# Raw weights in whole rows, and loads on other queues, in a hybrid attention and retention layer

## The chip, the core and the metric

The kernel runs on one core of a Trainium2 chip. The core has TensorE (PE, matrix products into PSUM), VectorE (DVE), ScalarE (ACT), GpSimd (POOL) and SyncE (SP), which run side by side and each in its own order, and 16 DMA engines that all queues share. SP, ACT and GpSimd can issue DMAs; an issue is an instruction in the stream of its engine. The metric is the device time of one execution in microseconds, lower is better.

## The reference

One decoder layer over 4096 tokens of width 1024, in float32:

```python
h = rms_norm(x, norm_gain)
proj = h @ w_in                       # 1024 x 3584
qa, ka, va, ga, qr, kr, vr, gr = split(proj, IN_SPLITS)
attn = dilated_attention(qa, ka, va)  # 8 heads x 64, rotary, three branches (128,1) (512,4) (2048,16)
ret = retention(qr, kr, vr)           # 4 heads, chunks of 128, decay, group norm
mixed = concat([silu(ga) * attn, silu(gr) * ret * ret_gn_gain])
out = rms_norm(x + mixed @ w_out, final_gain)
```

## The kernel before, in words

Products keep float32 accuracy by a split: each operand is a high part and a low part (operand minus high part), and three matmuls stand for one. ACT makes the high part, VectorE mostly the low one.

**Stage one** (`phase1`) makes q, k, the attention's v, and the retention's q and k. The columns of `w1` are taken in two passes, each over 8 blocks of 512 tokens: pass 0 (`ps` 0, blocks `q` 0 to 7) gives k and v, pass 1 (blocks 8 to 15) gives q and the retention's part. A block is not one product but seven smaller ones (P1, P5, P6, P3, P7, P2, P4, a scheme of Strassen's kind) from sums of the quarters of weights and of x. The quarters of the weights are A and B (alternate 128 columns), each with an upper half of rows (`Aa`, `Ba`) and a lower one (`Ab`, `Bb`). A product has two banks, thus a block 14 steps (`STEPS`) of 24 matmuls. What is done at which step is a list written by hand: `at(step, fn, ...)` appends a call, `front=True` puts it ahead of the step's others, and the loop at line 758 emits each step's product and then its calls. The order on each engine and queue is the order of these calls.

Before a pass the raw quarters lie in tiles that are free at that time (`ROOM`, line 191); from them `scale_b`, `minus` (GpSimd), `plus_times` (VectorE) and `split_w` make the operands of the seven products, and `HOMES` (line 206) says in which rooms the high and the low part of each are kept. At the start `load_w` (line 228) brings the quarters one by one, in pieces of 128 columns (512 bytes) and some of 256. For pass 1 `load_raw` (line 606) brings all four rows of a quarter with four or eight DMAs of 512-byte pieces, at steps s-13 and s-11 before the pass; the switch is at s = 112.

**The way into stage two** (s = 224): `first_k` loads the first head's K (4096 columns) on GpSimd's queue, `w2_some` the eight tiles of w2 on ACT's queue at s-10 and s-8, `w2_split` splits them, `first_chunk` and `first_chunk_split` bring and split the first two chunks of x, `first_q` loads q. **Stage two** (`phase2`) loads its constants on GpSimd's queue and then runs attention on TensorE, with the values and the retention as a `filler` between its steps; the filler runs alone first (`LEAD`, line 18). **Stage three** gates, projects and normalizes.

Of the kernel before, what the change touches and what calls it, by code (L numbers as in the profile page):

```python
# [24 lines left out]
S = 4096  # L25
# [113 lines left out]
def phase1(tc, io, dr, right, ahead):  # L139
# [5 lines left out]
    with ExitStack() as ctx:  # L145
# [41 lines left out]
        def whole(p, tag):  # L187
# [37 lines left out]
        def pairs_of(rows, c0, part):  # L225
            return rows[:, c0 : c0 + 512].rearrange("k (u t c) -> k t u c", t=2, c=128)[:, part]

        def load_w(ps, dst, part, k):

            rows = io["w1"][k * 128 : (k + 1) * 128, :]  # L230
            halves = [h.rearrange("k (u c) -> k u c", c=128) for h in (dst[:, 0:256], dst[:, 256:512])]
            nc.sync.dma_start(halves[0], pairs_of(rows, 0 if ps else 512, part))
            if ps:
                nc.sync.dma_start(halves[1], pairs_of(rows, 1024, part))
            else:
                nc.sync.dma_start(dst[:, 256:512], rows[:, 1536 + 256 * part : 1792 + 256 * part])
# [14 lines left out]
        def split_w(ps, prod, src, part=None, engine=None, ks=range(4)):  # L251
# [3 lines left out]
            for k in ks:  # L255
                hi, lo = W[ps].hi[prod][k], W[ps].lo[prod][k]
# [162 lines left out]
        def values(q, half):  # L419
# [3 lines left out]
            for i, p in enumerate(parts):  # L423
                for u in range(2):
                    n = 4 * q + 2 * half + u
                    nc.scalar.activation(
                        vf[:, u, 256 * i : 256 * i + 256], p[:, 256 * u : 256 * u + 256], AF.Copy, scale=rs[:, n : n + 1]
                    )
# [177 lines left out]
        def load_raw(name, room, part, k0):  # L606

            raw[name] = ROOM[room](F32)
            for i, t in enumerate(raw[name].tiles):
                n = raw[name].n  # L610
                r0 = (k0 + i * n) * 128
                for u in range(4):
                    c0 = (0, 1024)[u // 2] + 256 * (u % 2) + 128 * part
                    src = io["w1"][r0 : r0 + n * 128, c0 : c0 + 128]
                    nc.sync.dma_start(t[:, :, u * 128 : (u + 1) * 128], src.rearrange("(k p) c -> p k c", p=128))
# [98 lines left out]
        for k in range(4):  # L714
            load_w(0, Ab[k], 0, 4 + k)
# [1112 lines left out]
```

## Time and profile before

| | us |
|---|---|
| median of 3 runs | 2394.1 (2393.79 to 2399.23) |
| the profiled execution | 2397.46 |
| its span, first to last instruction | 2395.7 |
| TensorE busy in the span | 2287.0 (95%) |
| VectorE busy | 1734.7 (72%) |
| ACT busy | 1140.1 (48%) |
| GpSimd busy | 784.7 (33%) |
| mean granted TensorE clock | 0.980 |

Times in rows are us from the first instruction. Stage one lasts until about 739, stage two follows. A releaser (`<-`) is what ended a wait. q1 is SP's DMA queue, q10 ACT's, q0 GpSimd's. `ACTq` or `SPq` is an engine's DMA issue, with the time that it held the stream.

### The profile page before, as it was taken

What the parts mean: (1) busy time and instruction counts of PE and PEld (TensorE: products, weight loads), DVE (VectorE), ACT (ScalarE), POOL (GpSimd) and SP (SyncE); (2) the same over time, 40 slices, a digit from 0 to 9 for tenths busy, and PEclk for the clock granted to TensorE, in tenths of its full rate; (3) what the DMA queues carried; (4) which work ended last, traced back from release to release, by engine and by line L of the source; (5) the groups of instructions that cost most, each with busy time, mean ns of one, the idle gap of its engine ahead of it and who ended that gap; (6) DMA issues with size and microseconds to landing.
All of it is one profiled execution on the core that took longest, in us unless ns stands there. A gap on an engine that the chain in (4) does not pass through costs nothing.

```text
span 2395.7 us, 47366 instructions
## 1 busy us (share of the span) xinstructions
PE 2287.0 (95%) x16808; PEld 2059.8 (86%) x16808; DVE 1734.7 (72%) x4231; ACT 1140.1 (48%) x3082; POOL 784.7 (33%) x965
## 2 busy tenths in 40 slices
PE   5899997999986999999999999998899999999998
PEld 5899997999986888888888888877789999999997
DVE  6686778998976878787887879786655655555654
ACT  4555555332322666667666666667322322322221
POOL 1344443222122535344443535446121121121110
PEclk8999998999998999999999999999999999999999
DMA  6678777545467675858576675755676666666653
GB/s 185 203 234 260 229 239 211 163 153 178 152 184 205 139 171 138 188 125 192 139 167 153 153 165 127 178 136 184 156 185 152 148 169 147 143 171 152 141 156 93
DMA packets 457581, 405.07 MB, mean 169 GB/s; under 512 B 207896, under 2 KB 411800, under 8 KB 452224
## 3 DMA queue, kind: packets, MB, share of 16 engines
q1 hardware_dynamic: 421328, 324.52, 53.5%
q0 software_dynamic: 29968, 58.38, 8.3%
q10 hardware_dynamic: 6048, 19.14, 2.4%
q8 instruction: 133, 2.18, 0.4%
q14 instruction: 104, 0.85, 0.1%
HBM read 283.12 MB, written 118.64 MB: 168 GB/s over the span
## 4 chain that ended last, share of the span: by engine, by line
PE 59%; DVE 3%; DMA 3%; issue 1%; ACT 1%; SPq 1%; POOL 0%; POOLq 0%; DVEq 0%; ACTq 0%
PE S L1036 9%; PE O L1106 7%; PE T L1073 6%; PE po L48 4%; PE po L50 4%; PE po L49 4%; PE g L50 4%; PE g L49 4%; PE g L48 4%; PE V L48 3%; PE V L50 2%; PE V L49 2%; DMA wb<-dr_w 1%; PE Ro L1327 1%; PE Ro L1330 1%
## 5 line engine op out<-in xcount | busy, mean ns | idle before, releaser
L1057 DVE CUSTOM_DVE_ANT_0 S<-S,mask 128x256 f32<-128x256 f32 (+1 forms) x768 | 308.5, 402 | 158.8 <-PE S L1036 125.3
L1064 ACT ACTIVATE P<-S,nm 128x256 f32<-128x256 f32 (+1 forms) x768 | 338.0, 450 | 45.8 <-DVE nm L1057 42.7
L50 PE MATMUL g<-h,wg 128*128 128x256 f32 x1024 | 289.7, 283 | 0.0
L310 ACT ACTIVATE h<-xt 128x1024 fp32r<-128x1024 f32 (+1 forms) x115 | 119.4, 1038 | 240.7 <-DVE xt L302 107.3
L1073 PE MATMUL T<-ident,P 128*128 128x128 f32 x1368 | 213.2, 273 | 0.0
L49 PE MATMUL po<-wo,m 128*128 128x512 f32 x512 | 200.4, 391 | 0.0
L1617 POOL TENSOR_TENSOR rs<-v,mhalf 128x1 f32<-128x1 f32 x32 | 17.5, 547 | 546.6 <-DVE v L1615 527.6
L1106 PE MATMUL O<-pt,v 128*64 128x128 f32 (+1 forms) x1968 | 196.3, 326 | 0.0
L50 PEld LDWEIGHTS g<-h,wg 128*128 128x128 f32 x1024 | 196.2, 192 | 0.0
L1036 PE MATMUL S<-kk,qc 128*128 128x256 f32 x1024 | 187.6, 307 | 7.0 <-issue 2.8
L48 PE MATMUL po<-wohi,m 128*128 128x512 f32 x448 | 178.7, 399 | 6.4 <-ACT m L40 5.4
L1036 PEld LDWEIGHTS S<-kk,qc 128*128 128x128 f32 x1024 | 150.1, 191 | 35.7 <-issue 18.3
L50 PE MATMUL po<-wohi,m 128*128 128x512 f32 x448 | 176.7, 395 | 0.2 <-DVE m L41 0.2
L314 DVE TENSOR_TENSOR h<-xt,h 128x1024 fp32r<-128x1024 f32 (+1 forms) x115 | 138.8, 1207 | 49.5 <-ACT h L310 49.3
L1106 PEld LDWEIGHTS O<-pt,v 128*64 128x64 f32 x1968 | 121.3, 137 | 60.7 <-issue 31.6
L1556 ACT ACTIVATE e<-g 128x256 f32<-128x256 f32 x128 | 48.3, 379 | 256.1 <-PE g L50 239.7
L804 POOL TENSOR_TENSOR hc<-hr,hc 128x512 fp32r<-128x512 f32 x64 | 85.0, 1329 | 241.6 <-ACT hc L803 175.3
L1073 PEld LDWEIGHTS T<-ident,P 128*128 128x128 f32 x1368 | 163.7, 141 | 0.2 <-ACT wg0hi L87 0.2
L1064 ACT ACTIVATION_READ_ACCUMULATOR P<-S,nm 128x1 f32 x768 | 157.5, 205 | 0.0
L40 ACT ACTIVATE m<-e 128x256 fp32r<-128x256 f32 x128 | 53.1, 416 | 209.7 <-DVE e L1563 123.8
L48 PE MATMUL g<-h,wg1hi 128*128 128x256 f32 x512 | 145.2, 285 | 3.1 <-ACT e L1556 3.1
L49 PE MATMUL g<-h,wg1hi 128*128 128x256 f32 x512 | 146.1, 286 | 1.2 <-DVE h L852 1.0
(268 smaller groups left out, 6512.0 us busy)
## 6 DMA issues: line engine op xcount, KB each, us to landing
hr<-in_xT_dram SPq DMA_DIRECT2D x64, 512.0 KB
q<-dr_q SPq DMA_DIRECT2D x128, 256.0 KB
xt<-in_xT_dram POOLq DMA_DIRECT2D x60, 512.0 KB, 8.7
wb<-dr_w SPq DMA_DIRECT2D x128, 192.0 KB
o<-dr_o SPq DMA_DIRECT2D x192, 128.0 KB
v<-dr_v SPq DMA_DIRECT2D x94, 256.0 KB
xn<-in_x_dram ACTq DMA_DIRECT2D x32, 512.0 KB
dr_v<-vo SPq DMA_DIRECT2D x64, 256.0 KB
```

The lines of the kernel that those rows point to most:

```text
L40: nc.scalar.activation(dst[:, 0], src, AF.Copy)
L48: nc.tensor.matmul(out, wh, xh, start=first and i == 0, stop=False)
L49: nc.tensor.matmul(out, wh, xl, start=False, stop=False)
L50: nc.tensor.matmul(out, wl, xh, start=False, stop=last and i == n - 1)
L310: nc.scalar.activation(xs[q, prod][:, 0, ks, :], xq[(q, *SOURCE[prod])][:, ks, :], AF.Copy)
L314: (engine or nc.vector).tensor_tensor(h[:, 1, ks, :], src[:, ks, :], f32(h[:, 0, ks, :]), ALU.subtract)
L804: nc.gpsimd.tensor_tensor(hc[:, :, 1, :], src, hc[:, :, 0, :].bitcast(F32), ALU.subtract)
L1036: nc.tensor.matmul(s[:, j * 256 : (j + 1) * 256], qq[h, t, half][:, off : off + 128] if br == 0 else it["q"][:, t, i, :], rhs, start=(j == ...
L1057: nc.vector.tensor_tensor_reduce(sv, sv, mask[:, it["br"], c0:256], 1.0, BIG, ALU.add, ALU.min, accum_out=nm[:, col : col + 1])
L1064: nc.scalar.activation(it["P", i // 2][:, i % 2, c0:256], sv, AF.Exp, bias=nm[:, col : col + 1], scale=-1.0, accum_out=den[:, col : col + 1])
L1073: nc.tensor.transpose(t[:, j * 128 : (j + 1) * 128], it["P", bank][:, j // 2, j % 2 * 128 : j % 2 * 128 + 128], ident)
L1106: nc.tensor.matmul(o[64 * bank : 64 * bank + 64, c0 : c0 + 128 * m], vt[h, br, idx // 8][:, idx % 8, :], it["pt"][:, a : a + m, :].rearran ...
```

## The change

At the start and before pass 1 the raw weights come in rows of 512 columns (2 KB), A and B side by side in one tile (`Raw`); A and B are then views of it with 128-column pieces (`groups`). The upper halves come first, then the lower ones: for pass 1 at s-12, s-10 and s-8 rather than s-13 and s-11. The value columns of pass 0 are paired in another way, which `values` undoes. The products of pass 1 get other rooms, D lies in another one, and the sum S4 is written over Aa. The scaling of Bb moves from s-7 to s-6, and P1's split goes ahead of the first sum.

At the way into attention w2's loads go to SP's queue, all at s-10, and their splits to s-4 and s-3; K and q are loaded at first only in part (1024 of 4096 and 512 of 2048 columns), the rest on ACT's queue as the filler's first act; the constants go from GpSimd's queue to SP's, at the same place; the loads of x chunks 1 to 3 go from SP's to GpSimd's; and the first two v loads from GpSimd's queue to SP's, in chunk 1.

```diff
             {
-                "P5": ("wh0", "wl0"),
-                "P6": ("wh1", "wl1"),
-                "P3": ("h0", "h1"),
-                "P7": ("q00", "q10"),
-                "P2": ("q01", "q11"),
-                "P4": ("p40", "p41"),
+                "P5": ("wl0", "wl1"),
+                "P6": ("h1", "q10"),
+                "P3": ("h0", "p41"),
+                "P7": ("wh0", "wh1"),
+                "P2": ("q00", "q11"),
+                "P4": ("p40", "q01"),
             },
...
+        def groups(ap):
+            return ap.rearrange("p (g c) -> p g c", c=128)
+        COLS = ((512, 1536), (0, 1024))
+        class Raw:
+            def __init__(self, ps, rooms, k0):
+                self.ps, self.k0 = ps, k0
+                self.tiles = [t[:, i : i + 2, :] for r in rooms for t in ROOM[r](F32).tiles for i in range(0, t.shape[1], 2)]
+                both = [t.rearrange("p q (u t c) -> p (q u) t c", t=2, c=128) for t in self.tiles]
+                self.A, self.B = ([t[:, :, i, :] for t in both] for i in range(2))
+            def load(self, k):
+                for i, c0 in enumerate(COLS[self.ps]):
+                    nc.sync.dma_start(self.tiles[k][:, i, :], io["w1"][(self.k0 + k) * 128 : (self.k0 + k + 1) * 128, c0 : c0 + 512])
...
         def diff_d():
-            raw["D"] = ROOM["q01"](F32)
+            raw["D"] = [groups(t) for t in ROOM["q00"](F32)]
...
-            raw["S4"] = ROOM["q00"](F32)
-            plus_times(raw["S4"], raw["Ab"], 1, raw["Bb"], ALU.add)
+            plus_times(raw["Aa"], raw["Ab"], 1, raw["Bb"], ALU.add)
...
-        at(s - 13, load_raw, "Ba", "wh1", 1, 0, front=True)
-        at(s - 13, load_raw, "Aa", "wh0", 0, 0, front=True)
-        at(s - 11, load_raw, "Ab", "p40", 0, 4, front=True)
-        at(s - 11, load_raw, "Bb", "h0", 1, 4, front=True)
+        at(s - 12, load_raw, "a", range(4), front=True)
+        at(s - 12, open_raw, "a", ("wh0", "wh1"), 0, front=True)
+        at(s - 10, load_raw, "b", (0, 1), front=True)
+        at(s - 10, open_raw, "b", ("p40", "q01"), 4, front=True)
+        at(s - 8, load_raw, "b", (2, 3), front=True)
         at(s - 8, diff_d)
-        at(s - 7, lambda: scale_b(raw["Bb"]))
+        at(s - 6, lambda: scale_b(raw["Bb"]))
+        at(s - 6, split, 1, "P1", "Aa", 0)
         at(s - 6, sum_s1)
-        at(s - 6, split, 1, "P1", "Aa", 0)
...
-            ahead["w2"].load(raw["w2"], js, nc.scalar.dma_start)
+            ahead["w2"].load(raw["w2"], js)
...
-            ahead["kk"] = load_k(nc, kka, dr, 0, nc.gpsimd.dma_start)
+            ahead["kk"] = load_k(nc, kka, dr, 0, nc.gpsimd.dma_start, slice(0, 1024))
...
-            ahead["hr"] = load_x_chunk(nc, hcp, io, 1)
+            ahead["hr"] = load_x_chunk(nc, hcp, io, 1, nc.gpsimd.dma_start)
...
-        at(s - 10, w2_load)
-        at(s - 10, w2_some, (0, 1, 2))
-        at(s - 8, w2_some, (3, 4, 5, 6, 7))
-        for i in range(4):
-            at(s - 6 + i, w2_split, (2 * i, 2 * i + 1))
+        at(s - 10, w2_some, range(8), front=True)
+        at(s - 10, w2_load, front=True)
+        for i in range(2):
+            at(s - 4 + i, w2_split, range(4 * i, 4 * i + 4), front=True)
         at(s - 6, first_chunk)
-        at(s - 3, first_q)
+        at(s - 2, first_q)
         at(s - 2, first_chunk_split)
...
-        Aa, Ab, Ba, Bb = (ROOM[r](F32) for r in ("q11", "p41", "wl0", "h1"))
+        X, Y = Raw(0, ("h1", "q10"), 0), Raw(0, ("q11", "p41"), 4)
+        Aa, Ba, Ab, Bb = X.A, X.B, Y.A, Y.B
         for k in range(4):
-            load_w(0, Aa[k], 0, k)
+            X.load(k)
             load_x(0, 0, 0, k)
         load_x(0, 0, 1)
         for k in range(4):
-            load_w(0, Bb[k], 1, 4 + k)
-            load_w(0, Ba[k], 1, k)
-        load_x(0, 1, 1)
-        for k in range(4):
-            load_w(0, Ab[k], 0, 4 + k)
-        load_x(0, 1, 0)
+            Y.load(k)
+        for half in (1, 0):
+            load_x(0, 1, half)
...
-        for _ in range(2):
-            load_v(*vqueue[vpos[0]], nc.gpsimd.dma_start)
-            vpos[0] += 1
+        def first_loads():
+            load_constants()
+            for i in range(2):
+                load_q(nc, qp, dr, 0, i, 0, nc.scalar.dma_start, slice(512, S // 2), qq[0, i, 0])
+            load_k(nc, kka, dr, 0, nc.scalar.dma_start, slice(1024, S), kk[0])
...
             res = {0: first_rk}
+            first_loads()
             split_rk(first_rk)
...
-                        hraw[c + 1] = load_x_chunk(nc, hcp, io, c + 1)
+                        hraw[c + 1] = load_x_chunk(nc, hcp, io, c + 1, nc.gpsimd.dma_start if c < 3 else None)
```

## Rows read from the trace of the kernel before

**Rows 1.** Windows: busy us (count) of PE, PEld, DVE, ACT, POOL; clock, DMA share, GB/s

```profile
0.00:120.00 120.00, 89.33 (x591) 83.83 (x592) 76.39 (x97) 60.17 (x94) 31.57 (x46) 0.89 0.65 193
...
120.00:360.00 240.00, 238.22 (x1968) 234.65 (x1967) 179.68 (x215) 133.67 (x203) 103.98 (x155) 1.00 0.78 241
...
360.00:420.00 60.00, 45.63 (x309) 44.75 (x308) 48.22 (x65) 31.84 (x50) 22.20 (x32) 0.80 0.71 211
...
700.00:780.00 80.00, 55.01 (x352) 49.38 (x351) 48.66 (x96) 20.88 (x45) 21.93 (x29) 0.85 0.80 203
...
780.00:1300.00 520.00, 518.51 (x4076) 435.79 (x4075) 414.07 (x1545) 358.14 (x1238) 236.35 (x272) 1.00 0.66 155
```

**Rows 2.** Waits of TensorE from 700 to 780: total us, times, longest

```profile
PE V L50 <- POOL hc L804: 8.5, 2, 5.7
...
PE z L402 <- ACT m L410: 6.5, 1, 6.5
...
PE V L48 <- ACT vch L1405: 5.5, 1, 5.5
```

**Rows 3.** Timeline of ACT and VectorE at the end of stage one: start, us, what

```profile
697.87 11.46 ACTq L74 DMA_DIRECT2D w<-in_w_dram  x3
...
709.37 1.09 ACT L410 ACTIVATE m<-z 128x512 f32<-128x512 f32 x2 [10.46 <-DMA dr_r<-or]
...
715.10 5.70 ACTq L74 DMA_DIRECT2D w<-in_w_dram  x4
...
722.85 0.69 DVE L415 TENSOR_TENSOR m<-z,m 128x512 f32<-128x512 f32 x1 [6.35 <-ACT m L410]
```

**Rows 4.** DMA queues from 694 to 704 us: packets, MB, share of 16 engines

```profile
q0 software_dynamic: 178, 1.92, 90.2%
...
q10 hardware_dynamic: 62, 0.13, 5.7%
```

**Rows 5.** Windows at the end of stage one, columns as in rows 1

```profile
703.50:739.30 35.80, 27.07 (x195) 26.59 (x194) 19.20 (x31) 11.24 (x18) 2.58 (x5) 0.86 0.83 223
...
722.80:756.40 33.60, 23.14 (x146) 20.73 (x146) 31.22 (x51) 11.14 (x19) 7.60 (x11) 0.88 0.70 183
```

**Rows 6.** Timeline of SP's issues, and SP's queue from 729 to 740

```profile
727.14 3.92 SPq L909 DMA_DIRECT2D q<-dr_q  x8
...
q1 hardware_dynamic: 353, 1.86, 77.2%
```

**Rows 7.** Timeline of ACT and VectorE at the start

```profile
14.17 0.72 ACT L261 ACTIVATE w1wh<-w1q,gain_all 128x512 fp32r<-128x512 f32 x1 [0.23 <-DMA w1q<-in_w_dram]
...
21.15 2.33 DVE L314 TENSOR_TENSOR h<-xt,h 128x1024 fp32r<-128x1024 f32 x1 [3.84 <-ACT h L310]
...
23.39 1.75 DVE L267 SCALAR_TENSOR_TENSOR w1w<-w1w,gain_all,w1hc 128x512 f32<-128x512 f32 x1
...
26.50 0.75 DVE L267 SCALAR_TENSOR_TENSOR w1w<-w1w,gain_all,w1hc 128x512 f32<-128x512 f32 x1
```

**Rows 8.** DMA queues: SP's from 346 to 356, ACT's from 720 to 725

```profile
q1 hardware_dynamic: 3385, 1.68, 64.5%
...
q10 hardware_dynamic: 555, 1.01, 58.9%
```

**Rows 9.** Timeline at the switch of weights, and its window from 372 to 407.5

```profile
371.74 1.33 ACT L275 ACTIVATE w1hc<-w1hc,gain_all 128x512 f32<-128x512 f32 x2 [0.56 <-DMA w1hc<-in_w_dram]
...
377.32 1.22 DVE L314 TENSOR_TENSOR h<-xt,h 128x1024 fp32r<-128x1024 f32 x1
...
379.29 0.77 PE L402 MATMUL x<-h,w1q 128*128 128x256 f32 x2 [7.19 <-ACT w1wh L258]
...
372.00:407.50 35.50, 21.13 (x113) 20.35 (x113) 33.19 (x48) 18.39 (x31) 14.27 (x24) 0.70 0.62 183
```

**Rows 10.** Timeline of VectorE: low halves in scattered and in plain order

```profile
397.10 2.14 DVE L507 TENSOR_TENSOR hl<-o,hl 128x512 fp32r<-128x512 f32 x2
...
702.65 1.29 DVE L505 SCALAR_TENSOR_TENSOR hl<-o,hl 128x512 fp32r<-128x512 f32 x2
```

More of the change, by code (lines that the diff above doesn't have):

```diff
@@ L215, in phase1, with load_b @@
             {
-                "P5": ("wh0", "wl0"),
-                "P6": ("wh1", "wl1"),
-                "P3": ("h0", "h1"),
-                "P7": ("q00", "q10"),
-                "P2": ("q01", "q11"),
-                "P4": ("p40", "p41"),
-            },
-        )
[L225 to L236, printed above, removed]
+                "P5": ("wl0", "wl1"),
[4 more added lines that the diff above has]
+                "P4": ("p40", "q01"),
+            },
+        )
+        def groups(ap):
[10 more added lines that the diff above has]
+                    nc.sync.dma_start(self.tiles[k][:, i, :], io["w1"][(self.k0 + k) * 128 : (self.k0 + k + 1) * 128, c0 : c0 + 512])
+        def load_b(ps, dst, k):
+            rows = io["w1"][(4 + k) * 128 : (5 + k) * 128, :]
+            for i, c0 in enumerate(COLS[ps]):
+                src = rows[:, c0 : c0 + 512].rearrange("k (u t c) -> k t u c", t=2, c=128)[:, 1]
+                nc.sync.dma_start(groups(dst)[:, 2 * i : 2 * i + 2, :], src)
         def f32(ap):
@@ L604, in phase1, with open_raw, load_raw @@
         raw = {}
[L606 to L615, printed above, removed]
+        def open_raw(name, rooms, k0):
+            raw[name] = Raw(1, rooms, k0)
+            raw["A" + name], raw["B" + name] = raw[name].A, raw[name].B
+        def load_raw(name, ks):
+            for k in ks:
+                raw[name].load(k)
         def diff_d():
-            raw["D"] = ROOM["q01"](F32)
+            raw["D"] = [groups(t) for t in ROOM["q00"](F32)]
             minus(raw["D"], raw["Aa"], raw["Ba"])
@@ L638, in split_p4 @@
             t = raw["again"][:, k % 2, :] if k < 2 else raw["again2"][:, k % 2, :]
-            load_w(1, t, 1, 4 + k)
-            raw["P4", k] = t
+            load_b(1, t, k)
+            raw["P4", k] = groups(t)
         def split_p4_end(k):
@@ L659, in phase1 @@
         at(s - 2, split, 1, "P6", "Bb")
-        at(s + 1, split, 1, "P3", "S4")
+        at(s + 1, split, 1, "P3", "Aa")
         at(s + 3, split, 1, "P7", "D", 0)
@@ L680, in first_k @@
         def first_k():
-            ahead["kk"] = load_k(nc, kka, dr, 0, nc.gpsimd.dma_start)
+            ahead["kk"] = load_k(nc, kka, dr, 0, nc.gpsimd.dma_start, slice(0, 1024))
         def first_q():
-            ahead["qq"] = {(0, i, 0): load_q(nc, qp, dr, 0, i, 0) for i in range(2)}
+            ahead["qq"] = {(0, i, 0): load_q(nc, qp, dr, 0, i, 0, None, slice(0, 512)) for i in range(2)}
         def first_chunk():
@@ L753, in phase1 @@
             6: lambda: (square(0, 2), split_w(0, "P2", Ab, 1)),
-            7: lambda: ([load_w(0, Bb2[k], 1, 4 + k) for k in range(4)], square(0, 3), root(0)),
-            8: lambda: (split_w(0, "P4", Bb2, 1), load_n(1, 1)),
+            7: lambda: ([load_b(0, Bb2[k], k) for k in range(4)], square(0, 3), root(0)),
+            8: lambda: (split_w(0, "P4", [groups(t) for t in Bb2], 1), load_n(1, 1)),
             10: lambda: (along_free(0), copy_rb(0)),
@@ L908, in load_q @@
             p0 = dup * 64 + part * 32
-            dma(t[p0 : p0 + 32, :].bitcast(F32), dr["q"][i, part, h, :, half * 2048 : (half + 1) * 2048])
+            dma(t[p0 : p0 + 32, cols].bitcast(F32), dr["q"][i, part, h, :, half * 2048 + cols.start : half * 2048 + cols.stop])
     return t
```

27 lines of the change are left out of this document (14 added, 13 removed).

## The prediction

> **What bounds the kernel now.** I read the busy time by stretch first. TensorE is the bound in nearly all of the run: 238.2 of 240 us are busy from 120 to 360, 518.5 of 520 from 780 to 1300. Three stretches are not so, and the change touches just these: the start (89.3 of 120, clock 0.89), the switch to the second half's weights (45.6 of 60, clock 0.80), and the way from the first stage into attention (55.0 of 80, clock 0.85) [rows 1]. What is won or lost there stays to the end, since TensorE is full behind each of them. The lists of waits then say who holds TensorE, and the timeline why.
>
> At the way into attention TensorE waits 6.5 us for ACT's copies of its banks, later 5.5 us for ACT's first values and 8.5 us in two waits for GpSimd's half of an x chunk [rows 2]. ACT is late because it issues DMAs: three loads of w2 hold its stream from 697.9 for 11.46 us, and only at 709.4 it copies the bank; the next issue, of four, takes 5.70 us, and VectorE stands 6.35 us until 722.85 [rows 3]. The loads can't get in: from 694 to 704 GpSimd's queue, with the first head's K in rows of 16 KB, has 90.2% of the DMA engines and ACT's queue 5.7% [rows 4]. So from 703.5 to 739.3 TensorE does 195 matmuls in 35.8 us; at 238.22/1968 = 0.121 us each they are 23.6 us [rows 1, 5]. VectorE, idle before, is busy for 31.2 of the 33.6 us after 722.8: the tail that releases the first scores runs at VectorE's pace [rows 5].
>
> **The way into attention.** w2's eight loads go from ACT to SP at step -10 of this end (steps are counted from the end of the last block), ahead of two groups of four stores; only 1024 of 4096 K columns are loaded before attention (0.5 MB for 2 MB, rows of 4 KB). Eight issues cost SP 8 x 0.49 = 3.9 us (3.92 us for the eight q loads [rows 6]), and who waits behind them are stores, whose readers come much later. w2 is due at step -4, six half products or 6 x 24 x 0.121 = 17 us after. ACT's two stops, and VectorE's 6.35 us behind the second, have no cause left. TensorE's own loss there is 35.8 - 23.6 = 12.2 us [rows 1, 5]. VectorE's tail begins with the join at 722.85 [rows 3]; this join belongs to step -6, which begins one product (48 x 0.121 = 5.8 us) after 703.5; with ACT's copy ahead of it it can begin near 709.8, or 13.0 us earlier. The tail keeps its length, since the w2 splits only change places in it. I take 13.0, the larger, because the tail releases the first scores. Next late is again VectorE, not a DMA.
>
> Against this stand new issues. ACT gets twelve loads (eight of q, four of K, 3 MB in rows of 6 and 12 KB) as the filler's first act; at 0.49 us that is 5.9 us of ACT time. Behind them on ACT are the halves of the next chunk and the first values. While VectorE's tail runs ACT mostly waits, so this is hidden; without the cover it costs up to 5.9. The bytes are the other matter: q loads in rows of 8 KB moved 1.86 MB in 11 us [rows 6], so 3 MB take some 15 to 18 us in which small rows on other queues get little, as [rows 4] shows. Behind them now are the constants on SP (moved from GpSimd, due with the first scores), the stores of the last block, and x chunk 1 on GpSimd. Bounds: 0, if the burst lies in VectorE's tail, to 10, if it lies on the first scores. I charge 1.5, nearer to the cover, since all targets are free by then. GpSimd loses the five constants and two v loads in front of its chunk halves, and gets three chunk loads. The 2.8 us of [rows 2] that the constants caused lie ahead of VectorE's tail and give nothing. The two v loads on SP are due only with the first outputs, and cost nothing while SP's issues are short. Sum: -13.0 + 1.5 = **-11.5, bounds -16 to -2**.
>
> **The start.** Before, A's first tile (256 KB) and x's tile lead the queue; the fourth tile of A comes at 14.17 [rows 7]. Now A and B of a tile come together, so the four steps of P1 need 2.5 MB rather than 1.5. The price of a packet decides. Where SP's queue held almost only 512-byte packets, 3385 took 64.5% of 16 engines over 10 us, or 30.5 ns each; where ACT's held 2 KB packets, 555 took 58.9% over 5 us, 85 ns [rows 8]. Four small ones are 122 ns: 30% is saved per byte. The extra 1 MB is 512 packets x 85/16 = 2.7 us, and the saving on the first 1 MB is about 1 us; so the fourth step comes some 1.7 us later, of which TensorE, busy with the first three, hides a part. I count +0.7. On the other side B lies there when A does, so GpSimd's differences no longer run beside VectorE's low half of x (2.33 us, against 1.22 undisturbed [rows 7, 9]) and the first sum (1.75, against 0.75 [rows 7]): -2.0, if they are over by 21. **-1.3, bounds -3 to +3.**
>
> The Trainium skill prices small packets too ("DMA: Bandwidth & Descriptors", "Why small descriptors are slow (HBM only)"): some 3 cycles per packet on top of one for 32 bytes. By that estimate four of 512 bytes save 12%, not 30%, and the 4 MB of the next part would take 2.9 us more; the sum would be 2387.5. The rows here say 30%.
>
> **The switch of weights.** ACT waits for B's lower half, the last of it at 371.74; then sums, P1's split and the low half of x for P4 follow on VectorE, done at 377.32 + 1.22; TensorE, idle for 7.19 us, starts at 379.3. From there VectorE is busy for 33.2 of 35.5 us [rows 9], so a delay of it is a delay of the end. Now the stores of values go ahead of the first load (A and B upper, step -12), then half of the lower rows at step -10, the stores of k at -9, and the other half at -8, when P6's room is free. Before the last of lower B stood 4 MB (2 upper, 1 of stores, 1 of B); now stand 6 MB (A's lower half and the k stores come ahead too). By [rows 8] the three MB of small packets before were 6144 x 30.5/16 = 11.7 us. The four MB in 2 KB packets are 2048 x 85/16 = 10.9, and the k stores, 1 MB in 1 KB pieces, lie between both prices, 2.7 to 3.9, say 3.2. So 14.1 - 11.7 = 2.4 us later, less some 0.4 for stores that fill the queue earlier: +2. Order costs too: the scaling of B, P1's split and then the sum stand in a row behind the last tile, where before half of the sums ran before it came. One scaling and one high part on ACT at some 0.65 (0.72 for one [rows 7]), four splits and four sums on VectorE at some 0.7 (0.75 for one [rows 7]) and 1.22 make 8.1 us from B to P4's input, where it was 377.32 + 1.22 - 371.74 = 6.8: +1.3. **+3.3, bounds 0 (2 KB packets hold their share beside GpSimd's) to +7.** Homes of products are renamed at no cost: each new room is read out for the last time before it is written, by the same two engines in the same order.
>
> **Sum.** -11.5 - 1.3 + 3.3 = -9.5: the profiled execution (2397.5 us) would be 2388.0. It lies 3.4 above the median of 2394.1, so the median becomes **2384.6**.
>
> **Rivals.** (1) The burst at the entrance lies on the first scores: constants or the q columns from 512 on land late, because large rows starve small ones [rows 4, 6]. It gives back 8 more: -1.5, 2392.6. For it: the twelve loads are issued last; against it: their targets are free earlier. (2) VectorE's tail isn't freed, because another wait (w2 behind stores on SP, the tables) holds it: then only the 6.5 us of TensorE's wait for ACT [rows 2] come back, less 1.5, and +2 from start and switch: -3.0, 2391.1. (3) The entrance gains nothing. Three queues share 16 engines, and the same bytes come a little later: -1.3 + 3.3 = +2, 2396. The 11.46 us that ACT stood for three issues speak against it [rows 3].
>
> The Trainium skill has this as a rule ("DMA: Bandwidth & Descriptors", "Issuing engines are not separate DMA queues"): issuing from several engines saves only issue time, usually small. Here that time was 11.46 us.
>
> (4) Slower: the halves of raw tiles now lie in pieces of 128 columns. VectorE's low part in a scattered order took 2.14 us for two, 1.07 each, where the same in plain order took 1.29, 0.65 each [rows 10]. If pieces cost that, the switch has 32 such operations on VectorE (three sums and five splits of four) and the start 28 on the path: 60 x 0.42 = 25, +15.7 in all, 2409.8. It decides from about 0.28 us per operation on. Against it: the pieces are whole, only the steps between them are not.
>
> **Chances.** Forecast 0.60, (1) 0.14, (2) 0.11, (3) 0.05, (4) and the like 0.10. By 0.3% (7.2 us, about what can be told from no change) the forecast is faster, (1) to (3) are the same, (4) is slower: 0.60, 0.30, 0.10. The range is 2374 (all terms near their good bounds) to 2396 (rival 3); it leaves out rival 4 and a tail below.
>
> **What would show it.** At the entrance no DMA issue of w2 on ACT, TensorE through its last four products in about 24 us, VectorE's tail starting near 710, and the twelve loads over before the first scores. At the switch TensorE's wait before P4 some 3 us longer. At the start GpSimd's differences finished before VectorE's low half. The prediction is wrong if TensorE's idle time between 700 and 780 stays above 20 us, if ACT stands in its twelve issues, or if the 128-column operations take over 0.9 us.

## The result: slower by half a percent

The changed kernel takes 2406.76 us (median of 5 runs, 2404.67 to 2414.8) against 2396.45 for the kernel before in the same comparison: ratio 1.0053, interval 1.0031 to 1.0075. That is 7 to 18 us slower, where 9.5 less was forecast; the profiled execution has a span of 2403.1 us against 2395.7.

The windows of the profile after, columns as in [rows 1], with one stretch of 9 us added:

```profile
0.00:120.00 120.00, 91.43 (x625) 85.11 (x626) 79.18 (x104) 62.85 (x99) 33.58 (x49) 0.91 0.65 198
...
360.00:420.00 60.00, 35.54 (x251) 34.75 (x250) 41.84 (x58) 27.01 (x43) 21.20 (x31) 0.80 0.57 176
700.00:780.00 80.00, 47.55 (x325) 43.85 (x324) 46.17 (x81) 18.24 (x34) 16.74 (x20) 0.82 0.85 209
744.00:753.00 9.00, 0.00 (x0) 0.00 (x0) 3.96 (x9) 0.15 (x1) 2.11 (x3) 0.50 0.45 143
780.00:1300.00 520.00, 518.51 (x4070) 435.81 (x4070) 413.62 (x1540) 356.79 (x1234) 239.08 (x274) 1.00 0.65 153
```

Against [rows 1] TensorE has 2.1 us more in the first 120, 10.1 less at the switch, 7.5 less at the way into attention, and the same behind it. Its waits from 700 to 800:

```profile
PE V L48 <- ACT vch L1416: 23.7, 1, 23.7
PE S L1043 <- ACT P L1071: 7.1, 1, 7.1
```

ACT's first values, 5.5 us of waiting in [rows 2], now hold TensorE for 23.7 us.

**How the places are compared.** All kernels here issue the same 16 808 matmuls in the same order. I take the time at which one numbered matmul starts, minus its time in the trace of before: number 480 (99.7 us in before) closes the start, 2500 (353.3) to 5000 (679.4) holds the switch, 5000 to 5680 (799.8) the entrance. One trace is not exact. Where a kernel leaves a place as it was, the place still differs from before's trace: the start by 0, -0.8, -1.7 and -2.8 (mean -1.3), the switch by 0, -0.5, -0.7 and -0.7 (mean -0.5), the entrance by 0, +1.8, +2.0 and +4.4 (mean +2.05). Below, a place is held against these means; for whole kernels the ratios of the timed runs count. Ratios come from six comparisons, in which before's median lay between 2396.5 and 2402.0, so I take two ratios of different comparisons as comparable to about 0.2% (5 us).

### The profile page after: what moved, and what is told of

It reads as the page before. It is cut to its first block, busy times and chain, and to the rows that moved or that the text cites. A ratio compares the mean times of both kernels' runs of the same rounds, so it can differ in the third digit from the quotient of the medians.

```text
span 2403.1 us, 47344 instructions
## 1 busy us (share of the span) xinstructions
PE 2276.7 (95%) x16808; PEld 2049.9 (85%) x16808; DVE 1736.7 (72%) x4231; ACT 1140.5 (47%) x3082; POOL 785.3 (33%) x961
```

## The three parts alone

Three kernels are before with one part of the change each; a fourth has the start and the switch together.

> The kernel before, with the whole rows of A and B (and the layout of the values that goes with them) in the first half's weights alone; the switch and the entrance are before's. In fifteen traces with this start the products stand 1.0 to 3.5 us earlier by matmul 480 (mean 2.7). Theory (that is all it does, and it stays to the end): ratio 0.998 to 0.9996. Rival (the start's gain is lost in the full stretch behind it, as some traces drift by 3 to 4 us there): 0.9996 to 1.0012.

> The kernel before, with the new raw weights of the second half alone (whole rows, new homes, new steps, order of after); start and entrance are before's. Seven traces with this order lose 4.0 to 6.6 us from before the switch to matmul 5000 (mean 5.3). Theory (that is the whole price of the raw weights): ratio 1.0014 to 1.003. Rival (the switch costs more than the traces place there, which would explain that start and switch together measured 1.0042): above 1.003.

> The kernel before, with the changes at the entrance alone; start and switch are before's. Three traces with the rest of K and q on ACT lose 4.0 to 6.9 us there (mean 5.6). Theory (the entrance loses on its own): ratio 1.0014 to 1.003. Rival (it loses only because the first stage arrives late from the switch, and gains without that): 0.999 or below.

> The kernel before, with only the change to the raw weights, at the start and at the switch; the entrance is before's. If the three places add up as the two traces place them (start -3.1, switch +5.5), 2396.5 + 2.4 = 2399, range 2397 to 2401. Rival (what the entrance of after lost is an echo of the later arrival from the switch): 2404 to 2407.

The edit of e18, in short (e16 and e17 are the two halves of the rest of the diff, e3 both):

```diff
-            ahead["w2"].load(raw["w2"], js, nc.scalar.dma_start)
+            ahead["w2"].load(raw["w2"], js)
...
-            ahead["kk"] = load_k(nc, kka, dr, 0, nc.gpsimd.dma_start)
+            ahead["kk"] = load_k(nc, kka, dr, 0, nc.gpsimd.dma_start, slice(0, 1024))
```

| kernel | ratio to before (interval) | us | the place in its trace, less the mean of traces that leave it |
|---|---|---|---|
| e16, start | 0.9996 (0.9983 to 1.0010) | -1.0 | -1.2 (mean of 16 traces) |
| e17, switch | 1.0052 (1.0032 to 1.0071) | +12.5 | +5.9 (mean of 8) |
| e18, entrance | 1.0002 (0.9989 to 1.0015) | +0.5 | +2.7 (mean of 4, 0.2 in its own) |
| e3, start and switch | 1.0042 (1.0025 to 1.0060) | +10.1 | |
| after | 1.0053 (1.0031 to 1.0075) | +12.7 | +7.4, the sum of the three above |

The us are the ratio times 2399. The three parts add up to after: -1.0 + 12.5 + 0.5 = 12.0 against 12.7. So the forecast failed at two places: the entrance gives nothing where 11.5 was forecast, and the switch costs more than 3.3. e16 fell on the border of its two readings and e18 between them; e17 is its rival's, dearer than the traces show, and e3 came out at its rival's time (2405.27 us, before 2397.15), though not by an echo at the entrance: that is +1.8 there, within what unchanged entrances show.

## The switch

> The kernel after, with one step swapped at the switch: P1's split (it needs only A's upper half) stands ahead of the scaling of B on ACT and VectorE, not behind it. Theory (part of the switch's loss is order: VectorE waits 18.6 us for P1's high half while A has been there since 363): the split runs by 367, what is left behind B's last tile is one scaling, two sums and the low half of x, TensorE's wait before P4 of block 7 falls from 15.2 to about 11, and all behind it is 3 to 4.5 us earlier than in after: 2402 to 2404 against 2406.8. Rival (only B's arrival counts, the order is hidden): the wait stays within 1 us of 15.2 and the time is after's.

```diff
-        at(s - 6, lambda: scale_b(raw["Bb"]))
         at(s - 6, split, 1, "P1", "Aa", 0)
+        at(s - 6, lambda: scale_b(raw["Bb"]))
```

The timeline of after at the switch, ACT, VectorE and TensorE:

```profile
375.57 0.72 ACT L288 ACTIVATE w1q<-w1q,gain_all 128x512 f32<-128x512 f32 x1 [0.58 <-DMA w1q<-in_w_dram]
376.20 2.54 ACT L274 ACTIVATE w1kk<-w1wh,gain_all 128x512 fp32r<-128x512 f32 x4
...
376.94 2.74 DVE L275 SCALAR_TENSOR_TENSOR w1kk<-w1wh,gain_all,w1kk 128x512 fp32r<-128x512 f32 x4 [18.55 <-ACT w1kk L274]
...
380.93 1.40 DVE L280 SCALAR_TENSOR_TENSOR w1wh<-w1wh,gain_all,w1q 128x512 f32<-128x512 f32 x2
...
384.21 0.77 PE L415 MATMUL x<-h,w1q 128*128 128x256 f32 x2 [15.25 <-DVE m L428]
```

and the same with P1's split ahead:

```profile
374.68 0.72 ACT L288 ACTIVATE w1q<-w1q,gain_all 128x512 f32<-128x512 f32 x1 [1.55 <-DMA w1q<-in_w_dram]
...
375.49 0.75 DVE L280 SCALAR_TENSOR_TENSOR w1wh<-w1wh,gain_all,w1q 128x512 f32<-128x512 f32 x1 [1.52 <-ACT w1q L288]
...
378.12 0.77 PE L415 MATMUL x<-h,w1q 128*128 128x256 f32 x2 [9.99 <-DVE m L428]
```

The path is to be read from the last scaling of B on ACT to P4 on TensorE: 8.64 us in after (375.57 to 384.21), 3.44 with the split ahead. In before it was 6.9: the scaling behind the arrival at 371.74 takes 1.33 for two, the second begins near 372.4, P4 at 379.29 [rows 9]. So after's order costs 1.7 (forecast: 1.3), and since VectorE stands idle for 18.55 us before the split, putting the split into that idle time gives back 5.2. Five more kernels have this swap and no other change to after's switch; in the six traces the switch is at +0.4 on average against the unchanged (-0.3 to +1.0), where eight traces with after's order have +5.9 (+4.4 to +7.3). Three pairs of kernels differ by the swap alone. By the two ratios it is worth 10 us from after to e5 (1.0053 and 1.0010, 0.9999 to 1.0021), 7 from e2 to e9 and 3 from e8 to e12. The theory of e5 is borne out, and its 3 to 4.5 us were rather too few.

What is left of the 8 us by which P4 came late is the arrival: the last scaling is 6.3 us later against the products (375.57, with the products 3.1 early, against 372.4). SP's first loads of the chain that ends there, in before and then in after:

```profile
343.45 9.03 SPq L615 DMA_DIRECT2D w1wh<-in_w_dram  x8
```

```profile
345.91 10.90 SPq L242 DMA_DIRECT2D w1wh<-in_w_dram  x8
```

The chain is 29.0 us long in before (343.45 to 372.4) and 29.7 in after (345.91 to 375.57), but it begins 5.6 later against the products. The next kernel has P1's split ahead and begins it a step earlier.

> The kernel after with P1's split ahead, and the loads of A and B upper at step -13 again (ahead of the stores of values) instead of -12. In after the chain from the first of these loads to the last scaling of B was 29.7 us, in before 29.0, but it began 5.6 us later against the products. Theory (the lower half of B is late because its queue starts a step later, not because of more bytes): with the chain begun some 5 us earlier the last scaling comes 4 to 5 us earlier, TensorE's wait before P4 falls from 10.0 to 5 or 6, the switch as a whole ends 3 to 5 us below that of the kernel with P1's split ahead. Rival (between 355 and 365 the engines are full at 375 GB/s: bytes decide): the last scaling comes at most 1.5 us earlier, the wait stays above 8.5.

```diff
-        at(s - 12, load_raw, "a", range(4), front=True)
-        at(s - 12, open_raw, "a", ("wh0", "wh1"), 0, front=True)
+        at(s - 13, load_raw, "a", range(4), front=True)
+        at(s - 13, open_raw, "a", ("wh0", "wh1"), 0, front=True)
```

The timeline of this kernel, SP, ACT and TensorE:

```profile
340.15 5.92 SPq L242 DMA_DIRECT2D w1wh<-in_w_dram  x8
...
371.92 0.72 ACT L288 ACTIVATE w1q<-w1q,gain_all 128x512 f32<-128x512 f32 x1 [0.60 <-DMA w1q<-in_w_dram]
...
375.36 0.77 PE L415 MATMUL x<-h,w1q 128*128 128x256 f32 x2 [6.57 <-DVE m L428]
```

Against the products (each shifted by its matmul 2500, -3.3 here and -4.0 in e5, where the loads begin at 345.76) the loads begin 6.3 us earlier than in e5 and the last scaling comes 3.4 earlier; TensorE's wait falls from 10.0 to 6.6. That is between the two theories: about half of the late arrival is the step at which the queue begins, the other half is bytes or what holds SP's issues, which stays open. The time doesn't settle it (1.0012, 0.9998 to 1.0027), since this kernel's entrance was the worst of all (+4.8 against the unchanged).

A second kernel with the same edits at the switch, e14 below, confirms the earlier arrival but not that it lasts. Its last scaling comes 3.2 earlier than in e5 and TensorE's wait is 6.8; yet by matmul 5000 e13 stands at -3.1 against the unchanged and e14 at +0.3. Behind P4 they differ in the granted clock: from 395 to 405 it was 0.83 in e13 and 0.67 in e14.

## The way into attention: who was late next

Two things were to be told apart: whether what TensorE and VectorE win there stays, and what the rest of K and q costs. Three lines of before are the marks: ACT's first values, the last step of VectorE's tail (the high half of the retention's k), ACT's first probabilities.

```profile
752.39 0.67 ACT L1405 ACTIVATE vch<-V,rs_all 128x512 f32<-128x512 f32 x1
...
771.77 0.35 ACT L1064 ACTIVATE P<-S,nm 128x128 f32<-128x128 f32 x1
...
756.04 0.29 DVE L1276 CAST rkh<-rk 128x256 fp32r<-128x256 f32 x1
```

> The kernel before, with the eight loads of w2 moved from ACT to SP at step -10 and its splits moved as in after; K and q stay whole and early, raw weights, constants and chunks as before. Theory of the prediction (ACT's stop in three loads costs 12 us of TensorE and releases VectorE's tail): the last products of the first stage end 10 to 12 us earlier, and of this 8 to 12 us stay to the end: 2385 to 2389 against 2397. Rival (behind the tail stands a chain over GpSimd: the second chunk's load, its split, the first probabilities; it is bound by transfers, not by TensorE): TensorE ends its products earlier but first probabilities begin within 3 us of before's 771.8: 2393 to 2397.

It is before with the first line of the diff above and the moved splits of w2. Ratio 0.9994 (0.9977 to 1.0011): by its time the rival, though its first probabilities come a little earlier than the 3 us that the rival allowed. Its four last products end 12.5 us earlier against the products before them, as forecast (12.2). VectorE's tail ends 8.8 earlier (748.42, the products being 1.2 later). But ACT comes to the first probabilities only 4.9 earlier:

```profile
767.50 0.63 ACT L802 ACTIVATE hc<-hr 128x512 fp32r<-128x512 f32 x1 [17.60 <-DMA hr<-in_xT_dram]
768.04 0.35 ACT L1063 ACTIVATE P<-S,nm 128x128 f32<-128x128 f32 x1
```

They stand behind the split of chunk 2, and that waits 17.6 us for its DMA. At matmul 5680 1.2 us are left, or 3.3 against the mean of unchanged entrances.

The next four keep after's other edits and move the rest of K and q, or the stores beside it:

> The kernel after, with the twelve loads of the rest of K and q issued by SP instead of ACT, at the same place. Theory (ACT's stream is held between its own issues, and the halves of chunk 1 and the first values stand behind them): ACT splits chunk 1 when its data is there, near 741 instead of 758.8, the first values follow, TensorE's wait of 23.7 us before the second chunk's values shrinks below 10, and the run takes 10 to 16 us less than after: 2391 to 2397 against its 2406.8. Rival (the 3 MB in large rows are the price, whoever issues them): chunk 1 and the constants still come late, TensorE still waits some 20 us, 2403 to 2408.

> The kernel after, with K and q of the first head loaded whole at the old early places (K on GpSimd, q on SP) and no rest to load: what remains of the change at the entrance is w2 on SP, the constants, the x chunks and the v loads on their new queues. Theory: without the twelve issues the 12 us that TensorE won in its last products stay won: before's 2396.5, +2.4 for start and switch as the two traces show, -10 to -13, 2386 to 2389. Rival (the way in was bound by something else all along, w2 on SP only moves the wait): 2396 to 2400.

> The kernel after, the twelve loads still on ACT, but the sixteen stores of turned values of the last block (SP, eight of them in 9.6 us from 739.8 to 749.4, at some 95 packets of 1 KB a us) go to GpSimd's queue. Theory A (ACT's next issue is held while SP's slow stores are being taken in): ACT is through its loads near 750 instead of 758.8, 7 to 10 us less than after: 2397 to 2400. Theory B (ACT's issues hold themselves up, by its own queue's rows): ACT is through no earlier than 756, and the time stays within 3 us of after's 2406.8.

> The kernel after, with each of the last block's stores of turned values (128 rows of 1 KB, 4 heads x 32) written as four stores of one head (32 rows), still on SP; the twelve loads stay on ACT. Theory (a store with four heads outermost keeps only some 4 of 16 DMA engines busy: 95 GB/s and a busy share of 0.28 from 744 to 753, and ACT's next issues wait meanwhile): the stretch of 0.28 vanishes, ACT is through its twelve loads before 753 instead of 758.8, 5 to 9 us less than after: 2398 to 2402. Rival (32 issues on SP take as long as the eight did, or ACT's hold has another cause): ACT ends after 756, 2404 to 2410.

```diff
e1: -   load_k(nc, kka, dr, 0, nc.scalar.dma_start, slice(1024, S), kk[0])
    +   load_k(nc, kka, dr, 0, None, slice(1024, S), kk[0])
e2: -   load_k(nc, kka, dr, 0, nc.scalar.dma_start, slice(1024, S), kk[0])
    +   ahead["kk"] = load_k(nc, kka, dr, 0, nc.gpsimd.dma_start)
e4: +   put = nc.gpsimd.dma_start if q == NB2 - 1 else nc.sync.dma_start
e7: +   for h in range(4):
    +       nc.sync.dma_start(dst[h], src[32 * h : 32 * h + 32])
```

(The last block has eight such stores, not the sixteen of e4's expectation.) The timeline of after shows what they are about, ACT and SP, and then the DMA queues from 744 to 753 (packets, MB, share of 16 engines):

```profile
731.33 9.66 ACTq L916 DMA_DIRECT2D q<-dr_q  x3
...
743.54 0.31 ACTq L916 DMA_DIRECT2D q<-dr_q  x1
750.48 8.29 ACTq L821 DMA_DIRECT2D kk<-dr_k  x4
758.82 0.63 ACT L810 ACTIVATE hc<-hr 128x512 fp32r<-128x512 f32 x1 [14.67 <-DMA dr_q<-hl]
759.35 0.67 ACT L1416 ACTIVATE vch<-V,rs_all 128x512 f32<-128x512 f32 x1
...
739.83 9.58 SPq L493 DMA_DIRECT2D dr_r<-or  x8
```

```profile
q1 hardware_dynamic: 869, 0.87, 29.5%
q10 hardware_dynamic: 74, 0.42, 15.4%
```

One issue on ACT takes 0.31 us, yet the twelve are spread from 723 to 758, and behind the last stand chunk 1's half and the first values, at 759.35. VectorE's tail was over at 747.7, 10.8 us earlier than in before; the values are 4.4 later. From 744 to 753 the DMA engines are less than half busy, SP's queue with stores of 1 KB rows at 869 packets in 9 us.

**What an issue waits for.** The semaphores in the trace's records of the issues tell what the timeline doesn't (a semaphore is a counter that one instruction raises and another waits for). In these programs a DMA that was issued by SP or ACT raises one of eight semaphores when it has landed. The eight go round over the issues of both engines together, and an issue first waits until the DMA that had its semaphore last, eight issues earlier, has landed. GpSimd's DMAs have eight others. In after, eight of ACT's twelve issues start 0.02 us behind such a landing, seven of them that of a DMA of SP:

| ACT's issue at | starts behind the landing of | which SP had issued at |
|---|---|---|
| 729.46 | a load of q | 726.94 |
| 731.33 | a constant (`rgain`) | 728.57 |
| 735.72 | a constant (`cdec`) | 730.82 |
| 740.69 | a store of q (L525) | 737.47 |
| 750.48 | a store of turned values (L493) | 741.79 |
| 757.36 | a store of turned values (L493) | 748.17 |
| 757.99 | a store of q (L525) | 749.52 |

So ACT isn't held by its own issue time, nor because two engines issue at once, but until stores of SP have landed: 8.7 and 9.2 us for the two of turned values. Before had this already: the third load of [rows 3] starts at 708.99, 0.02 us behind the landing of a store that SP had issued at 693.28.

| kernel | rest of K and q | first values | first probabilities | entrance, less unchanged | ratio (interval) |
|---|---|---|---|---|---|
| after | 3 MB late, ACT | +4.4 | +2.4 | +2.0 | 1.0053 (1.0031 to 1.0075) |
| e5, e13, e18 | 3 MB late, ACT | +5.8, +3.7, +4.0 | +3.5, +2.1, -0.3 | +3.8, +4.8, +0.2 | 1.0010, 1.0012, 1.0002 |
| e7, stores in quarters | 3 MB late, ACT | +7.9 | +1.5 | +1.1 | 1.0015 (0.9999 to 1.0031) |
| e4, stores on GpSimd | 3 MB late, ACT | +1.0 | -4.4 | -6.4 | 1.0016 (0.9999 to 1.0032) |
| e1 | 3 MB late, SP | -13.0 | -10.8 | +1.6 | 1.0047 (1.0024 to 1.0071) |
| e15 | 3 MB late, GpSimd | -4.0 | -7.4 | -4.2 | 0.9984 (0.9968 to 1.0000) |
| e8, e12 | 1.5 MB (q) late, SP | -9.4, -9.9 | -7.5, -8.5 | -3.8, -4.6 | 0.9996, 0.9983 |
| e2 | none late | -10.6 | -5.1 | -7.2 | 1.0008 (0.9993 to 1.0023) |

(Columns 3 and 4: us against before, each trace shifted by its own matmul 5000; of the "less unchanged" column the 2.05 above is taken off. Three more traces have before's entrance, e3, e16 and e17: there the first values come at -5.0, -1.0 and -4.3, the first probabilities at +0.9, +0.4 and +2.8, so these marks scatter by some 5 and 3 us without any edit there.)

**e1** is the instructive miss. ACT issues nothing, the first values come 13.0 us earlier and the first probabilities 10.8, as the theory wanted, and the end gains nothing: its time (2405.82) is its rival's. The timeline, ACT, SP and GpSimd, and a line of TensorE's waits:

```profile
743.02 0.67 ACT L1416 ACTIVATE vch<-V,rs_all 128x512 f32<-128x512 f32 x1
764.55 0.35 ACT L1071 ACTIVATE P<-S,nm 128x128 f32<-128x128 f32 x1
...
766.50 7.06 SPq L1273 DMA_DIRECT2D rq<-dr_r  x1
...
778.12 0.73 POOL L1284 TENSOR_TENSOR rkl<-rk,rkh 128x256 fp32r<-128x256 f32 x1 [12.07 <-DVE rkh L1283]
...
PE S L1043 <- ACT P L1071: 9.7, 4, 3.8
```

Now SP is the stream that is held: a load of the retention's q takes 7.06 us to get in, GpSimd waits 12.07 us for what follows from it, and TensorE waits 9.7 us in four pieces for probabilities. The wait moved from ACT to SP. **e4** gained what theory A forecast (2400.7), but not by its mechanism: ACT's last issue was over at 758.6, where A said near 750. Six of the twelve issues still start behind a landing, of loads, constants or ACT's own, and two of the last take 3.25 and 1.61 us themselves. Without the slow stores the queues fill the engines from 744 to 753, 94% instead of 45%, and the data behind come earlier:

```profile
q1 hardware_dynamic: 2083, 1.26, 54.9%
q10 hardware_dynamic: 82, 0.52, 20.5%
q0 software_dynamic: 424, 0.39, 18.4%
```

**e7** is its rival's in the trace: in quarters SP issues a store of 32 rows every 0.46 us at best, which is no more than 70 rows a us, and ACT's issues waited longer, to 764. The last four, for K, start behind the landing of quarters issued at 746.50, 751.84, 757.98 and 760.30. These land within 1.6 to 3.7 us, but there are now 32 of them in the round. By the ratio e7 is 9 us below after, which is the theory's time and which its trace doesn't explain. So it can't tell whether the four heads outermost make the eight slow; that stays open. **e2**, with nothing late, has the entrance of the theory (-7.2) but the time of the rival (2397.61, before 2397.15): the switch, as in after, takes it back.

> The kernel after with P1's split ahead, and the twelve loads of the rest of K and q on GpSimd's queue, the third queue to have them (ACT: entrance +4 to +6 us against before; SP: +3.6). Theory (that 3 MB are asked for after 723 is the price, whichever engine issues them): entrance +2 to +7. Rival (the price is the place in the two queues that the hardware serves alike, SP's and ACT's; GpSimd's lies outside): entrance -2 or better.

> The kernel after, with K of the first head whole and early on GpSimd's queue as in before, and the rest of q (eight loads, 1.5 MB) on SP behind the constants; ACT issues none of the first head's loads. Theory (what costs is 3 MB asked for between 723 and 760, when the second chunk, the constants and the stores want the same engines): half of it goes while the engines are little used, nothing holds ACT, and the constants aren't behind q: entrance 5 to 10 us better than before's, 2389 to 2395. Rival (K's rows of 16 KB starve w2, which now is on SP, and give it back): like the kernel with both whole, 2396 to 2399.

> The kernel after with P1's split ahead, K whole and early, the rest of q on SP behind the constants. It differs from the kernel with both mends in 1.5 MB of q alone, which come at 731 to 757 instead of 728 to 737. Theory (late bytes are the price of the change at the entrance): 2 to 4 us above the kernel with both mends. Rival (which of the two is late does not count as long as ACT issues none): within 1.5 us of it.

e15 is e5 with another queue for the rest (`nc.gpsimd.dma_start`), so e5 is its partner; e8 has K whole and the rest of q on SP, and e12 is e8 with P1's split ahead. e15, GpSimd's issues and TensorE's longest wait:

```profile
729.73 1.97 POOL L916 DMA_DIRECT2D q<-dr_q  x4
731.70 1.45 POOL L821 DMA_DIRECT2D kk<-dr_k  x3
...
PE V L48 <- ACT vch L1416: 12.4, 1, 12.4
```

GpSimd puts seven of the loads in within 3.4 us, 0.49 each: the DMAs that had their semaphores before have all landed. (The twelfth, at 736.01, does wait, for a load that GpSimd itself had issued at 728.80.) The same 3 MB at the same place in the program give -4.2 from this queue, and +0.2 to +4.8 from ACT's or SP's; against e5 alone it is -4.2 for +3.8, and a ratio of 0.9984 (0.9968 to 1.0000) for 1.0010. That is the rival's reading (-2.1 against before, where it said -2 or better). The rival's "place in the two queues" is, by the trace, the round of eight semaphores that SP and ACT share. Bytes count for some 3 us (none late -7.2, e15 -4.2), the waits for landings for the rest, each from a trace or two. e4 says the same from the other side: it takes the stores out of the round instead of the loads. e8 and e12, with half the bytes late, lie between in their traces; in its time e8 (2399.78 with before at 2402.02) falls between its two readings, and e12 (2393.95 beside e9's 2394.09) is its rival's. The Trainium skill ("DMA: Bandwidth & Descriptors", "Issuing engines are not separate DMA queues") says that issuing from several engines saves only the time of the issue, which is usually small. Between ACT and SP that agrees (+2.0 and +1.6); from GpSimd (-4.2) more was saved here, the waits in front of the issues.

## The best of it together

> The kernel after with two mends: P1's split ahead of the scaling of B at the switch, and K and q of the first head whole at their old early places. By the traces of the runs that had one of the two: start -2 to -3, switch +0.5, entrance about -5, so 6 to 8 us less than before on the same chip (ratio 0.9967 to 0.9975). Rival (what the switch wins is taken back at the entrance, where the transfers decide and not TensorE): 1 to 3 us less than before (ratio 0.9988 to 0.9996).

> The kernel with both mends, and for the third chunk (number 2) alone the first half's split two products of 'values' later in ACT's and GpSimd's order. In all traces so far the first probabilities stand on ACT directly behind this split, which waits 15 to 21 us for the chunk's data. Theory (the order on ACT behind chunk 2's landing holds the first probabilities): they begin with the first scores, 5 us or more earlier than in the kernel with both mends, and the time falls 2 to 5 us. Rival (the transfers themselves are the bound: q's second half and chunk 2 land no earlier, and TensorE waits for them next): within 1.5 us of the kernel with both mends.

> The kernel with both mends, and the five constants back on GpSimd's queue at their old place, ahead of the first chunk's split, instead of on SP behind q. With K and q whole, GpSimd waited 7.1 us for one of them (qdec) and issued chunk 2's load only behind that, at 767.4. Theory (constants on SP behind q's rows of 8 KB hold GpSimd's chain): chunk 2's load is issued near 760, the first probabilities begin some 6 us earlier, the time falls 2 to 5 us below the kernel with both mends. Rival (chunk 2's data would come no earlier, since SP's queue fills the engines): within 1.5 us.

> The kernel with P1's split ahead, the upper loads at step -13, K and q whole and early, the constants on GpSimd's queue and the split of chunk 2's first half later: all mends at once. If they add up (start -3, switch -3 to -4, entrance -5 to -8) it is 11 to 15 us below before on the same chip, ratio 0.9937 to 0.9954. Rival (the mends at the entrance replace one another, and the switch is bound by bytes): like the best of them alone, ratio 0.996 to 0.9975.

```diff
e10: -   if k == HS and c < NCH - 1:
     +   if k == (7 if c == 1 else HS) and c < NCH - 1:
e11: -   nc.sync.dma_start(t, io[n])
     +   nc.gpsimd.dma_start(t, io[n])
```

| kernel | ratio to before (interval) | first probabilities | entrance, less unchanged |
|---|---|---|---|
| e9, P1 ahead, K and q whole | 0.9977 (0.9964 to 0.9991) | -5.5 | -7.6 |
| e10, and chunk 2's split later | 0.9969 (0.9956 to 0.9982) | -10.9 | -8.4 |
| e11, e9 and the constants on GpSimd, at their old place | 0.9970 (0.9957 to 0.9983) | -10.6 | -7.0 |
| e14, all and the upper loads earlier | 0.9969 (0.9955 to 0.9984) | -14.8 | -5.1 |

All four beat before by a clear interval, and so after; e10 is 7.4 us faster than before, some 20 faster than after by the two ratios. e9 is what its theory said, less a little. e10 began the probabilities earlier, as expected, but is only 1.8 us below e9 in the medians (2392.28 and 2394.09), between its two readings; e11 with 0.9 below is its rival's. They also show the next bounds in turn. In e9 GpSimd waits for a constant, and the first probabilities behind chunk 2; e10 takes chunk 2 out of ACT's way, and then VectorE reaches q's second half just as it lands (a line each of e9 and e10):

```profile
752.67 1.52 POOL L1313 TENSOR_TENSOR qg<-rq,qdec 64x256 f32<-64x256 f32 x2 [7.30 <-DMA qdec<-in_qdec_dram]
```

```profile
754.39 0.37 ACT L1071 ACTIVATE P<-S,nm 128x128 f32<-128x128 f32 x1 [16.31 <-DVE nm L1064]
...
769.42 1.35 DVE L1019 CAST qc<-q 128x512 fp32r<-128x512 f32 x1 [0.35 <-DMA q<-dr_q]
```

With the first probabilities 5.4 us earlier than e9, e10 keeps 0.8 of it in the trace; e14 begins them 14.8 earlier than before and ends no better. The mends don't add up: the rival of e14. Each takes away one late thing and meets the next.

## Why the prediction was wrong

**The start, -1.3, fits**: -1.0 by the runs, where the interval of e16 goes from -4 to +2.4 us and so can't tell it from no gain, and -1.2 by the traces, in which unchanged starts alone scatter by 2.8. Its two terms show in the timeline of after, against [rows 7]:

```profile
14.56 0.72 ACT L274 ACTIVATE w1wh<-w1q,gain_all 128x512 fp32r<-128x512 f32 x1 [0.76 <-DMA w1q<-in_w_dram]
...
20.37 1.23 DVE L327 TENSOR_TENSOR h<-xt,h 128x1024 fp32r<-128x1024 f32 x1 [1.49 <-ACT h L323]
21.51 0.74 DVE L280 SCALAR_TENSOR_TENSOR w1hc<-w1hc,gain_all,w1q 128x512 f32<-128x512 f32 x1
...
16.39 1.41 POOL L284 TENSOR_TENSOR w1q<-w1q 128x512 f32<-128x512 f32 x1 [0.63 <-DVE w1wh L275]
```

The fourth step comes 0.4 later (forecast 0.7); GpSimd's differences are over at 17.8, and the low half takes 1.23 for 2.33, the first sum 0.74 for 1.75: 2.1 (forecast 2.0).

**The switch, +3.3 with bounds 0 to +7, was mis-sized**: +5.9 by the traces, +12.5 (7.7 to 17) by the runs. The order term was right (1.7 for 1.3). The arrival term failed: 6.3 for 2. I had priced the bytes ahead of lower B. From the first load to the last scaling the chain is in fact hardly longer. It begins 5.6 later, because the loads went from step -13 to -12, behind the stores of values. I had named that move, and given it no time of its own. Moved back, it gives 3.4 (e13) and 3.2 (e14) of the arrival back; the rest of the 6.3 stays open. I also took the order as a thing to be priced rather than asked what could fill VectorE's idle 18.55 us; the swap showed that 5.2 lay there. Why the timed runs of e17 and e3 lose twice what their traces place at the switch stays open. The execution of e17 that was traced is the fastest of its six (2406.15, the others up to 2414.65). The mean granted clock was 0.976 to 0.981 in e17's runs and 0.977 to 0.983 in before's, which would fit stretches at the lower clock, but no trace of a longer run shows where.

**The entrance, -11.5, was wrong**: about 0. Of its steps, TensorE's 12.2 were 12.7 in after, and VectorE's 13.0 were 10.8. The step that failed is the sentence behind them, "Next late is again VectorE, not a DMA." The next late thing was ACT's own stream in after, chunk 2's DMA in e6, SP's stream in e1, a constant in e9, q's second half in e10. TensorE stood idle for 32 us between 700 and 780, where the prediction had set 20 as the sign of being wrong. With none of the rest late, 7 to 8 of the 10.8 can be kept (e2, e9, e10); with w2 on SP alone, 3.3 (e6).

**The twelve issues, +1.5 with bounds 0 to 10**: the three late-on-ACT traces beside after and after itself mean +2.7, none late -7.2 (e2), so the price was 9.9, at the far bound. I charged it near zero because "all targets are free by then", which is about their targets, and took an issue at 0.49 us. What counted was that an issue on ACT waits until the DMA eight issues earlier, mostly one of SP's, has landed, and that the first values stand behind it on ACT. The sign was there: three issues took 11.46 us on ACT [rows 3], and I put it to GpSimd's large rows keeping the loads out. The third waited for the landing of SP's store of 693.28; large rows may have made that landing late, but they didn't refuse the load.

**The rivals.** (1) had nearly the price (8) and the place, with a chance of 0.14, and a different cause (constants, for which no engine waits in after's trace from 700 to 800); (2) is refuted, since VectorE's tail was freed by 10.8; (3) had the entrance at nothing, with 0.05, but by bytes alone, which are some 3 of the 9.9. None of the three reached the slower side, because I let the switch stand at 3.3 in each. (4), the one that did, is refuted: two sums in pieces of 128 columns take 1.40 us and four low halves 2.74, as in plain order. "If ACT stands in its twelve issues" was rightly named as what would make the prediction wrong.

## What to carry to other kernels

A wait that is taken away is worth the distance to the next late thing, so follow the path on to where the bound engine is full again, naming at each in-order stream (ACT, SP, GpSimd) what stands in front; here the next one took back between a quarter and all of what VectorE's tail had won. Loads issued from a computing engine are priced by what stands behind them on that engine, and by the landings that they wait for, not by their own issue time; so look up in the trace which earlier DMA each issue waits for. And when an engine is idle ahead of a late arrival, ask which of the steps behind it need only what is there already: one swap of two lines was worth 5 us in the traces, and 3 to 10 by the ratios of three pairs.

## What was unexpected of the hardware

- What looked like a queue that doesn't take ACT's issues (0.31 us each, up to 7 us apart from 731.33 to 758.7 in after) were waits for landings that the program put there. GpSimd's seven, whose semaphores were free, took 0.49 each without a pause (e15).
- The last block's stores, 128 rows of 1 KB each with four heads outermost, landed as late as 8.7 and 9.2 us after their issue (after), while SP's queue moved some 97 packets a us with 29.5% of the engines. Stores of 32 rows landed within 1.6 to 3.7 us, but 32 of them took 19.2 us to issue (e7).
- While TensorE stood still for 23.7 us its granted clock was 0.50 (the 1.2 GHz level), in the whole of 744 to 753 (after).
